# All transfers of a streaming kernel in one DMA queue

## The chip, the cores and the metric

The kernel runs on one core of a Trainium2 chip. The metric is the device time of one execution in microseconds (us), the median of several. A profile adds the span from the first to the last instruction, which is some 1.8 us shorter here. For one core the runs can't be sorted by comparing dies, so a run is called slow only when it is over 1.5% above the fastest of its kernel.

## The reference

The input is float32, 8 x 4096 x 2112. Groups of four neighbouring rows are averaged, and the average is subtracted from each of the four.

```
x_r = x.reshape(B, S // 4, 4, D)
pooled = x_r.mean(axis=2)
upsampled = np.repeat(pooled, 4, axis=1)
return x - upsampled
```

Every byte is read once and written once: 276.82 MB each way.

## The kernel before

A tile is 128 groups, one for each partition: 33,792 contiguous bytes a partition, 4.325 MB in all. There are 64 tiles and 6 slots in on-chip memory. A slot is loaded, changed in place by VectorE, and stored. SyncE issues all loads, ScalarE all stores, so there are two queues. Each issue can carry a wait, and an issuer stands still at it.

```
for k in range(n):                       # n = 64
    b, lap = k % SLOTS, k // SLOTS       # SLOTS = 6
    ...
    load = nc.sync.dma_start(out=slots[b][:], in_=xg[tile_rows])
    if lap:
        load._wait_ge(store_sems[b], 16 * lap)
    load.then_inc(load_sems[b], 16)

    add = nc.vector.tensor_add(out=s[:], in0=rows[:, 0, :], in1=rows[:, 1, :])
    add._wait_ge(load_sems[b], 16 * (lap + 1))
    ...                                  # two more adds, one fused multiply-add over the slot

    store = nc.scalar.dma_start(out=og[tile_rows], in_=slots[b][:])
    store._wait_ge(done_sem, done)
    store.then_inc(store_sems[b], 16)
```

## Time and profile before

| quantity | kernel before |
|---|---|
| time, median of 6 runs | 1286.78 us (1286.73 to 1287.18) |
| span of the profiled run | 1285.0 us |
| VectorE busy | 1026.5 us, 80% |
| two DMA queues, share of 16 engines | 50.0% and 49.9% |
| moved | 553.67 MB, 431 GB/s over the span |

Read it from the shares: the DMA engines are full and VectorE is not. The time of this kernel is the number of bytes over the rate of the DMA engines, as long as nothing lets those engines run dry. The prediction below shows the lines.

### The profile page before, as it was taken

The numbers are of one execution on the slowest core, as the hardware profiler recorded it, in microseconds if no ns is written. First come the engines' busy times: TensorE is split into PE (matmuls) and PEld (weight loads), VectorE is DVE, ScalarE is ACT, GpSimd is POOL, SyncE is SP. The second block draws the span as 40 slices with busy tenths as digits, with TensorE's granted clock in tenths as the row PEclk, the third lists the DMA queues.
The fourth block names the chain that finished last, engine by engine and source line by source line (L and its number), as shares of the span: only waits on it lengthen the run. The fifth ranks groups of instructions, "written<-read, shape, count | busy, mean of one in ns | idle before, by whom it ended". The sixth has DMA issues, their size and how long they took to land.

```text
span 1285.0 us, 439 instructions
## 1 busy us (share of the span) xinstructions
DVE 1026.5 (80%) x256; POOL 0.2 (0%) x4
## 2 busy tenths in 40 slices
DVE  5998778787787877878778788787887878878774
POOL 0000000000000000000000000000000000000000
DMA  9999999999999999999999999999999999999998
GB/s 404 421 438 432 426 438 437 430 429 437 437 431 429 437 437 431 429 437 437 431 429 437 437 431 429 437 436 430 430 438 434 429 432 438 434 428 433 438 434 374
DMA packets 18434, 553.67 MB, mean 431 GB/s; under 512 B 2048, under 2 KB 2048, under 8 KB 2048
## 3 DMA queue, kind: packets, MB, share of 16 engines
q1 hardware_dynamic: 9216, 276.83, 50.0%
q10 hardware_dynamic: 9216, 276.83, 49.9%
q14 instruction: 2, 0.02, 0.0%
HBM read 276.82 MB, written 276.82 MB: 431 GB/s over the span
## 4 chain that ended last, share of the span: by engine, by line
DVE 80%; another core or an unknown queue 17%; DMA 1%; issue 0%; SPq 0%
DVE slot L75 45%; DVE s_ps L71 12%; DVE s_sb L71 12%; DVE s_ps L66 6%; DVE s_sb L66 6%; DMA slot<-in_x_dram 1%; SPq L118 0%; SPq L53 0%
## 5 line engine op out<-in xcount | busy, mean ns | idle before, releaser
L75 DVE SCALAR_TENSOR_TENSOR slot<-s_sb,slot 128x8448 f32<-128x8448 f32 x32 | 286.7, 8958 | 1.1
L75 DVE SCALAR_TENSOR_TENSOR slot<-s_ps,slot 128x8448 f32<-128x8448 f32 x32 | 286.6, 8957 | 1.1
L66 DVE TENSOR_TENSOR s_sb<-slot 128x2112 f32<-128x2112 f32 x32 | 75.5, 2358 | 123.4 <-DMA slot<-in_x_dram 123.4
L66 DVE TENSOR_TENSOR s_ps<-slot 128x2112 f32<-128x2112 f32 x32 | 75.7, 2367 | 113.0 <-DMA slot<-in_x_dram 113.0
L71 DVE TENSOR_TENSOR s_ps<-s_ps,slot 128x2112 f32<-128x2112 f32 x64 | 151.4, 2366 | 2.2
L71 DVE TENSOR_TENSOR s_sb<-s_sb,slot 128x2112 f32<-128x2112 f32 x64 | 150.9, 2358 | 2.2
L107 POOL MEMSET const-uint8-127<- 128x1 uint8 x1 | 0.1, 102 | 0.0
L107 POOL MEMSET const-bfloat16-1.0<- 128x1 bf16 x1 | 0.1, 101 | 0.0
L107 POOL MEMSET const-float32-0.0<- 128x1 f32 x1 | 0.1, 98 | 0.2 <-issue 0.2
L107 POOL MEMSET const-float32-1.0<- 128x1 f32 x1 | 0.1, 98 | 0.0
## 6 DMA issues: line engine op xcount, KB each, us to landing
slot<-in_x_dram SPq DMA_DIRECT2D x64, 4224.0 KB, 59.7
out_dram<-slot ACTq DMA_DIRECT2D x64, 4224.0 KB, 43.9
```

The source lines that it names most:

```text
L66: add = nc.vector.tensor_add(out=s[:], in0=rows[:, 0, :], in1=rows[:, 1, :])
L71: add = nc.vector.tensor_add(out=s[:], in0=s[:], in1=rows[:, f, :])
L75: sub = nc.vector.scalar_tensor_tensor(out=rows, in0=s[:, None, :].to_broadcast([P, STRIDE, D]), scalar=-1.0 / STRIDE, in1=rows, op0=mybir ...
L107: nc = _bacc.Bacc("TRN2", target_bir_lowering=False, num_devices=1)
```

## The change

Its intent is to give the transfers one fixed order, store and load in turn, in place of leaving it to the engines how they mix two queues. SyncE issues everything. The load that refills a slot is put one store later than it could be: behind the store of tile k comes the load that waits for the store of tile k-1. The diff, with unchanged lines cut:

```diff
         done = 0
+        done_at = []
         for k in range(n):
...
-            load = nc.sync.dma_start(out=slots[b][:], in_=xg[tile_rows])
-            if lap:
-                load._wait_ge(store_sems[b], 16 * lap)
-            load.then_inc(load_sems[b], 16)
...
-            store = nc.scalar.dma_start(out=og[tile_rows], in_=slots[b][:])
-            store._wait_ge(done_sem, done)
+            done_at.append(done)
+
+        def load(k):
+            b, lap = k % SLOTS, k // SLOTS
+            dma = nc.sync.dma_start(out=slots[b][:], in_=xg[k * P:(k + 1) * P])
+            if lap:
+                dma._wait_ge(store_sems[b], 16 * lap)
+            dma.then_inc(load_sems[b], 16)
+
+        for k in range(SLOTS):
+            load(k)
+        for k in range(n):
+            b = k % SLOTS
+            store = nc.sync.dma_start(out=og[k * P:(k + 1) * P], in_=slots[b][:])
+            store._wait_ge(done_sem, done_at[k])
             store.then_inc(store_sems[b], 16)
+            if k and k - 1 + SLOTS < n:
+                load(k - 1 + SLOTS)
 
-        for b in range(SLOTS):
-            nc.sync.wait_ge(store_sems[b], 16 * len(range(b, n, SLOTS)))
+        for k in range(n - SLOTS, n):
+            nc.sync.wait_ge(store_sems[k % SLOTS], 16 * (k // SLOTS + 1))
```

More of the change, by code (lines that the diff above doesn't have):

```diff
@@ L58 @@
             s = s_ps if k % 2 else s_sb
-            tile_rows = slice(k * P, (k + 1) * P)
-            load = nc.sync.dma_start(out=slots[b][:], in_=xg[tile_rows])
-            if lap:
-                load._wait_ge(store_sems[b], 16 * lap)
-            load.then_inc(load_sems[b], 16)
             add = nc.vector.tensor_add(out=s[:], in0=rows[:, 0, :], in1=rows[:, 1, :])
```

## The prediction

> **What bounds the kernel now.** I read the page from the top, then asked the trace for the same quantities in stretches of the run. The first thing is the busy row and the row of the DMA engines.
>
> ```profile
> DVE 1026.5 (80%) x256; POOL 0.2 (0%) x4
> ...
> DMA  9999999999999999999999999999999999999998
> GB/s 404 421 438 432 426 438 437 430 429 437 437 431 429 437 437 431 429 437 437 431 429 437 437 431 429 437 436 430 430 438 434 429 432 438 434 428 433 438 434 374
> ```
>
> VectorE is busy for 80% of the span and never full after the opening. The 16 DMA engines are at 90% or more in 39 of the 40 slices; only the first and the last slice move visibly less (404 and 374 GB/s). So the kernel streams, and VectorE is hidden behind the stream. The table of queues says who uses the engines:
>
> ```profile
> q1 hardware_dynamic: 9216, 276.83, 50.0%
> q10 hardware_dynamic: 9216, 276.83, 49.9%
> ...
> HBM read 276.82 MB, written 276.82 MB: 431 GB/s over the span
> ```
>
> q1 is SyncE's queue (the loads), q10 ScalarE's (the stores). Together their packets fill 99.9% of 16 engines for 1285.0 us: there is almost no idle engine time to win. Each queue has 9216 packets for 64 transfers; 128 rows of 33,792 bytes times 64 are 8192 data packets, and the other 1024 are 16 small semaphore packets for each transfer. One data packet takes about 0.500 x 16 x 1285.0 / 8192 = 1.255 us by this line (1.251 us in the packet records themselves, the same for loads and stores). An engine carries 8192 x 2 / 16 = 1024 of them, so 1024 x 1.251 = 1281 us of pure transfer in a span of 1285.0 us.
>
> The decisive view is the table of stretches, because the kernel already shows, at its two ends, what one queue alone can do. Columns are the stretch, its length, busy VectorE, busy GpSimd, clock, share of the DMA engines, GB/s:
>
> ```profile
> 14.00:29.00 15.00, 14.90 (x4) 0.00 (x0) 1.00 1.01 437
> 62.00:1253.40 1191.40, 962.09 (x240) 0.00 (x0) 1.00 1.00 433
> 1253.40:1278.00 24.60, 16.06 (x4) 0.00 (x0) 1.00 1.01 437
> ```
>
> From 14 to 29 us only loads run (the first store is issued at 29.51 us). From 1253.4 us only stores run: the last tile's first add starts at 1253.41 us, when the last load has landed. Both stretches, one queue each with several transfers end to end, show 437 GB/s; the middle with both queues shows 433. These figures count a packet whole in one stretch, so a short window is uncertain by a few GB/s. I read all three as one rate. A single queue, loads only or stores only, loses nothing at the joints between transfers.
>
> Last, the waits of the DMA issuers and the times to landing:
>
> ```profile
> SPq L61 <- DMA out_dram<-slot: 1170.2, 58, 50.6
> ...
> slot<-in_x_dram SPq DMA_DIRECT2D x64, 4224.0 KB, 59.7
> out_dram<-slot ACTq DMA_DIRECT2D x64, 4224.0 KB, 43.9
> ```
>
> SyncE spends 1170 us waiting for stores to free slots, 58 times, once for every load after the first six. This is no loss: a load takes 59.7 us from issue to landing and a transfer needs 4.325 MB / 433 GB/s = 10.0 us of all engines, so several transfers always stand in line. The wait is the queue being full.
>
> **What the Trainium skill says.** "DMA: Bandwidth & Descriptors", section "Issuing engines are not separate DMA queues": DMAs started by different engines run on the same 16 DMA engines, and several issuers save only the sequencer's issue time. The trace agrees: issuing is 0.33 us of a 20 us tile period, and one queue or two show 437 and 433 GB/s. The same page, "Where 436 GB/s comes from", gives 435.2 GB/s as the fabric's ceiling; the 433 here is within 1% of it. Its section "Queues, rings and completion order" says that an engine takes turns between queues by packet, takes one queue's descriptors in order, and that the semaphore increment is a write that lands only after that engine's earlier writes. The last could stall a queue; the stores-only stretch at 437 GB/s shows no such stall between stores. "HBM Reference", section "Specifications (TRN2)", says a core streaming alone is bounded by its 16 DMA engines, near 425 GB/s; this trace is a little above.
>
> **The change part by part.**
> Removed: 64 store issues from ScalarE. Added: the same 64 on SyncE, 0.34 us each, 22 us over the run on an engine that waits 1170 us. They cost nothing on the path. Bytes, packets and VectorE's 256 instructions are the same.
> Moved: order. SyncE now issues L0 to L5, S0, S1, L6, S2, L7, S3, L8 and so on, and stands still at whichever waits first: a store waits for VectorE, load k+5 for store k-1 to land. The question is whether the queue ever drains while SyncE stands still.
>
> Opening: the six loads run until 1.0 + 48 x 1.251 = 61 us. A tile takes VectorE 3 x 2.36 + 8.96 = 16.05 us, and the first result is ready at 29.5 us as now, so S0 is issued at 29.5 and S1 at 45.6 us, both before the loads end. S0 runs from 61 to 71, S1 to 81. Load 0's data take about 11 us and the first add starts at 13.34 us, so I estimate some 1.5 us from last byte to waiter. L6 is then issued at about 72.6, while S1 still has 8 us to run; S2 (ready since 61.6) follows it at once. No gap.
>
> Steady state: call t the moment when S(k-1) ends. The order S(k-2), L(k+3), S(k-1), L(k+4), S(k) puts S(k-2)'s end at t - 20. L(k+4) and S(k) are issued 1.5 us after that, at t - 18.5, while L(k+3) and S(k-1) are still in line. So the queue holds at least 18 us of work when new work comes. VectorE has tile k loaded at t - 70 and done by about t - 52, some 34 us before its store can be issued; it never holds SyncE up. Of a 20 us period it has 4 us free, as now.
>
> Tail: the last load goes before five stores, 50 us before the end. VectorE needs 16 us for it, so its store is ready long before its turn. Now, the last store is issued at 1269.6 us, while the one before is still running.
>
> The sum: at 433 GB/s the 553.65 MB take 1278.6 us. The other 6.4 us of the span are the first packets (0 to 10 us at 324 GB/s: 10 x (1 - 324/433) = 2.5 us), a small dip when the stores set in (29 to 62 us at 418 GB/s: 1.1 us), and the end (1270 to 1285 us at 324 GB/s: 3.8 us), rounded. The first is unchanged, since the same six loads are issued first. The dip may go, move or stay. Of the end, the data stop near 1282 us and the rest is the last receipt and the closing of the program, which the change keeps. So about 1 us can be won, and about as much lost. Reported time is 1.8 us above the span (1286.81 against 1285.0). I predict **1286.5 us**.
>
> **The rivals.**
> (a) Turning from load to store within one queue costs something. In the opening dip some 30 packets of q1 took 2.1 instead of 1.25 us, 0.85 us more. If every engine paid 0.85 us at each of some 120 turns, the time would rise by 102 us to about 1389 us. Against it: in the middle each engine already mixes equal numbers of load and store packets, and practically all take 1.251 us.
> (b) The semaphore write behind a store holds up the load behind it in the same queue. With two queues the other would fill that gap. At an estimated 1.5 us (the landing time above) for each of 58 joints this is 87 us, 1374 us. Against it: the stores-only tail passes such joints at full rate. But a store followed by a load in one queue is seen nowhere in this trace, so it isn't closed.
> (c) Head-of-line blocking: SyncE waits for one thing while another could go. For it: one issuer, two kinds of waits, both in strict order. Against it: 18 us in line and 34 us slack at VectorE. If the slack were wrong by a whole tile, VectorE (1026 us plus two unhidden ends) would come near the bound, some per cent slower.
> (d) Faster: fewer turns between reads and writes at the memory. The unmixed stretches read 437 against 433, at most 1% or 12 us, inside the counting error. The packet time is the same to the nanosecond in both, so I give it little.
>
> **Range and chances.** Runs before lie within 0.5 us. The floor of 1281 us plus start and receipt keeps the time above about 1284; small stalls from (a) or (b) would add a few us. Range 1284.5 to 1290. Beyond 2% slower (1312.5) only (a), (b) or (c) in full reach: 5% together. Faster by 2% would need 443 GB/s: 1%.
>
> **What would show it.** In the changed kernel's table of queues one queue should have 18,432 packets, 553.65 MB and about 99.9%; the table of stretches 433 GB/s through the middle; VectorE still 1026 us with waits of about 3.8 us for each tile. Times to landing show the new order: loads about 30 us (three transfers), stores about 40 us (four). SyncE's waits should still name stores, near 19 us each. Wrong by (a): longer packets at equal engine share and lower GB/s. By (b): a share well under 99%, with VectorE idle longer. By (c): SyncE waiting on VectorE and the DMA row below 9.

## The result, and the profile after

| | before | after |
|---|---|---|
| time, median of 6 runs each | 1286.78 us | 1288.27 us (1287.65 to 1289.08) |
| ratio of fast runs, 95% interval | | 1.0011 (0.9998 to 1.0024) |
| span of the profiled run | 1285.0 us | 1286.2 us |

The time is the same within 2%. A ratio here is the mean time of one kernel's fast runs over that of the other's of the same rounds, so it isn't quite the ratio of the medians.

The page of the changed kernel, the lines that answer to those of the prediction:

```profile
DVE 1026.0 (80%) x256; POOL 0.2 (0%) x4
...
DMA  9999999999999999999999999999999999999998
GB/s 404 420 433 430 430 435 433 432 432 435 434 433 432 433 435 434 433 431 435 434 432 432 435 434 432 431 433 435 435 432 432 434 435 431 432 435 435 431 433 372
...
q1 hardware_dynamic: 18432, 553.66, 99.9%
...
slot<-in_x_dram SPq DMA_DIRECT2D x64, 4224.0 KB, 29.9
out_dram<-slot SPq DMA_DIRECT2D x64, 4224.0 KB, 39.5
```

The row of DMA engines is the same, digit by digit, and one queue now holds what two held: 18,432 packets at 99.9%. Only the times to landing moved: loads from 59.7 to 29.9 us, stores from 43.9 to 39.5 us. They are times of standing in line. A shorter line with the same throughput moves no more data.

The waits of the issuer, after (waiter, what it waited for: total us, times, longest):

```profile
SPq L86 <- DMA out_dram<-slot: 1111.1, 58, 28.4
SPq L95 <- DVE slot L70: 85.5, 5, 25.7
```

SyncE waited 1111.1 / 58 = 19.2 us for each store, a little under one tile period of 20.0 us. It waited for VectorE only 5 times: twice at the opening, for the first two stores, while the first six loads were still running, and for the last three stores, issued at 1211.24, 1231.23 and 1251.17 us, when no load was left to issue. The last store came into line some 23 us before its turn, so this cost nothing.

The opening dip of the stream is still there, but later. The stretches before, then after:

```profile
29.00:62.00 33.00, 32.79 (x10) 0.00 (x0) 1.00 0.99 418
62.00:102.00 40.00, 39.16 (x12) 0.00 (x0) 1.00 1.00 433
```

```profile
29.00:62.00 33.00, 32.79 (x10) 0.00 (x0) 1.00 1.03 430
62.00:102.00 40.00, 39.69 (x12) 0.00 (x0) 1.00 0.97 418
62.00:1253.40 1191.40, 977.80 (x244) 0.00 (x0) 1.00 1.00 433
```

Before, stores join the loads at 29.5 us and the dip is there. After, the first store stands behind six loads and runs from some 61 us on, and the dip follows it. Over the middle the changed kernel holds 433 GB/s, as the kernel before does.

### The profile page after: what moved, and what is told of

It reads as the page before. It is cut to its first block, busy times and chain, and to the rows that moved or that the text cites. A ratio compares the mean times of both kernels' runs of the same rounds, so it can differ in the third digit from the quotient of the medians.

```text
span 1286.2 us, 437 instructions
## 1 busy us (share of the span) xinstructions
DVE 1026.0 (80%) x256; POOL 0.2 (0%) x4
## 3 DMA queue, kind: packets, MB, share of 16 engines
q1 hardware_dynamic: 18432, 553.66, 99.9%
## 4 chain that ended last, share of the span: by engine, by line
DMA 90%; DVE 7%; SPq 1%; issue 0%
DMA out_dram<-slot 86%; DVE slot L70 3%; DMA slot<-in_x_dram 3%; DVE s_ps L66 1%; DVE s_sb L66 1%; SPq L86 1%; DVE s_ps L61 1%; DVE s_sb L61 1%; SPq L128 0%; SPq L53 0%
## 6 DMA issues: line engine op xcount, KB each, us to landing
slot<-in_x_dram SPq DMA_DIRECT2D x64, 4224.0 KB, 29.9
out_dram<-slot SPq DMA_DIRECT2D x64, 4224.0 KB, 39.5
```

## The experiments

The theory: 16 DMA engines stream at one rate, whichever queue feeds them and in whichever order, as long as work stands in line. In one queue, what keeps work in line is where the waits sit in the order. The rivals from the prediction are that a turn between store and load costs time (a), that a semaphore write behind a store holds up its queue (b), that one wait in strict order blocks work that could go (c), and that one queue is faster (d).

### Is the 1.5 us real, and does the queue or a longer line matter? (e1, e3, e4)

e1 is the changed kernel again. e3 puts the load one store later still:

```diff
-            if k and k - 1 + SLOTS < n:
-                load(k - 1 + SLOTS)
+            if k >= 2 and k - 2 + SLOTS < n:
+                load(k - 2 + SLOTS)
```

e4 issues everything, the last waits too, from ScalarE:

```diff
-            dma = nc.sync.dma_start(...)
+            dma = nc.scalar.dma_start(...)
-            store = nc.sync.dma_start(...)
+            store = nc.scalar.dma_start(...)
```

> The changed kernel once more, to size a difference of about 0.1%. My theory (the 16 DMA engines stream at one rate whichever queue feeds them) expects a ratio of 1.000 to 1.002 to the kernel before, spans of 1285.5 to 1287.5 us. If the 1.5 us between the first medians was only the spread of runs, the interval should include 1.000 with a ratio below 1.0005; if it is real, the interval should lie above 1.0005.

> One queue, the load of tile k+4 behind the store of tile k (waits for the store two tiles back): more work in line. My theory expects no change: 1287 to 1289 us, DMA share 99.9%. If the last 1.5 us of the changed kernel come from a line that is sometimes nearly dry, this one should give them back, 1286.8 us.

> The changed kernel with all transfers and the last waits on ScalarE in place of SyncE. My theory expects the same as the changed kernel, 1287 to 1289 us, with all 18432 packets in q10. If SyncE's queue had something special, this one should differ by more than 2 us.

Measured, 5 runs each: e1 1288.15 us (1287.70 to 1288.55), e3 1288.07 us (1287.33 to 1290.51), e4 1288.20 us (1287.22 to 1288.92), beside 1286.83 us (1286.71 to 1287.16) of the kernel before. Ratios are 1.0009, 1.0012 and 1.0009, each with an interval from about 0.9997 to about 1.0023. So the interval does not separate one queue from two, and e1 fits neither of the two outcomes named before it: its ratio is above 1.0005, its interval includes 1.000. But of 15 one-queue runs none is as fast as the slowest of the 9 runs of the kernel before beside them: some 1.3 us are probably real, a tenth of a per cent. A longer line does not give them back (e3), and they don't belong to SyncE's queue (e4).

Where they sit can be seen at the end of the span. The kernel before, then the changed one; the last column is GB/s:

```profile
1281.00:1282.00 1.00, 0.00 (x0) 0.00 (x0) 1.00 0.09 34
1282.00:1283.00 1.00, 0.00 (x0) 0.00 (x0) 1.00 0.00 0
```

```profile
1281.00:1282.00 1.00, 0.00 (x0) 0.00 (x0) 1.00 0.24 101
1282.00:1283.00 1.00, 0.00 (x0) 0.00 (x0) 1.00 0.24 101
1283.00:1284.00 1.00, 0.00 (x0) 0.00 (x0) 1.00 0.08 34
```

34 GB/s in 1 us is one packet of 33,792 bytes. Before, one engine brings its last packet after 1281 us. After, several engines are still at work until past 1283 us: a few are late, not the stream as a whole. The records of single packets say more: after 100 us, 2 data packets of the kernel before took over 1.27 us, but 24 in the changed kernel, 60 in e1, 65 in e3 and 56 in e4. Many of them, above all early on, lie near the moments at which the queue turns between store and load. Worked out as an average over 16 engines, they add 0.5 to 0.8 us in place of 0.1 us, about half of what is to be explained. The rest is that the engines drift apart, and the end waits for the last of them. Each engine writes the semaphore once behind its part of a transfer, so these 16 writes show the spread. In the changed kernel they lie 0.7 us apart for the first loads, 2.8 us in the middle and 3.3 us for the last store (3.2 to 3.6 us in e1, e3 and e4); in the kernel before it is 0.4, 1.0 and 1.8 us. For the last store the first write comes at 1281.30 us, against 1281.20 us before, the last at 1284.58 us against 1282.99 us. Why an engine is now and then late at a turn is not shown, and stays open.

### Does the order matter at all? (e2)

e2 takes the shift by one store away: the load that refills slot k stands directly behind the store of tile k.

```diff
-            if k and k - 1 + SLOTS < n:
-                load(k - 1 + SLOTS)
+            if k + SLOTS < n:
+                load(k + SLOTS)
```

> One queue, but the load of tile k+6 stands directly behind the store of tile k and waits for it to land, so the later stores stand behind that wait. My theory (what keeps one queue full is the work already in line when SyncE stands still, which the shift by one tile in the diff gives) expects the line to run dry at each store: 2.5 to 3.5 us of landing and new start at each of 58 tiles, 1430 to 1490 us, and a DMA share near 87%. The rival (the order of issue in one queue does not matter, because the engines are the limit) expects 1286 to 1290 us.

Measured: 1511.77 us, ratio 1.1752 (1.1734 to 1.1770). The rival falls: order matters much. My size was too small (1430 to 1490 us), and so was the share (near 87%). The lines of e2's page and a piece of its timeline (start, length, engine, line, what):

```profile
span 1511.1 us, 437 instructions
...
q1 hardware_dynamic: 18432, 553.66, 92.3%
```

```profile
599.50 0.33 SPq L86 DMA_DIRECT2D slot<-in_x_dram  x1
599.88 0.43 SPq L95 DMA_DIRECT2D out_dram<-slot  x1
...
623.07 0.33 SPq L86 DMA_DIRECT2D slot<-in_x_dram  x1
623.44 0.43 SPq L95 DMA_DIRECT2D out_dram<-slot  x1
```

Load and store are issued as a pair, then nothing for 23.6 us until that store has landed. By then the queue is empty. The cost is 1511.1 - 1286.2 = 225 us, or 3.9 us for each of 58 refills. The share splits it: the engines' idle time rose from 0.1% of 1286.2 us to 7.7% of 1511.1 us, by 115 us, and their busy time from 1285 to 1395 us, by 110 us, although the bytes are the same. So each dry spell costs about 2.0 us of idle engines and another 1.9 us in which packets are in flight but take longer. I had counted only the first kind. The packet records after 100 us say where the second kind lies, as an average over the engines: about 0.6 us in the first packets after the restart, and 1.3 us some 8 to 11 us later, in the last packets of the load, before the store behind it begins. In this run the turn from load to store is not free. The run also shows that a busy share of DMA engines can hide a loss: 92.3% sounds better than 366 GB/s is.

This shows what the diff's "k - 1" does. With it, a store and a load stand in line while SyncE waits; the timeline of the changed kernel has the first refill issued while the second store still runs:

```profile
74.42 0.34 SPq L86 DMA_DIRECT2D slot<-in_x_dram  x1
74.80 0.63 SPq L95 DMA_DIRECT2D out_dram<-slot  x1
...
84.47 0.34 SPq L86 DMA_DIRECT2D slot<-in_x_dram  x1
```

The second refill could only be issued 10.05 us later, when the second store had landed: that store followed the first at full rate, so the line was never dry between.

### Does a turn cost, or a joint? (e5, e6, e11)

Each transfer is cut into four, one for each of the four rows of a group. In e5 the four stores of a tile are issued in a row, then the four loads. In e6 they alternate. Each quarter has a store semaphore of its own, and VectorE waits for all four loads. From e5 to e6 the edit is:

```diff
             more = k and k - 1 + SLOTS < n
             for f in range(STRIDE):
                 store(k, f)
-            for f in range(STRIDE):
                 if more:
                     load(k - 1 + SLOTS, f)
```

> One queue, each transfer cut into four of 8448 bytes a row, stores of a tile in a group of four, then the loads in a group of four: four times the transfers, joints and semaphore writes, four times the packets, but as many turns between store and load as the changed kernel has (some 120). My theory expects 433 GB/s and at most 1% over the changed kernel, 1288 to 1300 us. If the semaphore write behind a store held the queue up by even 0.2 us, 192 more joints behind stores would add some 38 us: 1326 us or more.

> The same quarters, but store and load alternate quarter by quarter: the same packets and semaphore writes as the grouped one, four times its turns (some 470). My theory (a turn costs nothing) expects the time of the grouped one within 3 us. The rival (each turn costs 0.85 us, the excess of the slow packets at the first turn) expects 350 turns more, 300 us more, about 1590 us; a turn cost of 0.05 us would show as 18 us.

Measured, 4 runs each: grouped 1303.78 us (1303.49 to 1304.14), ratio 1.0132; mixed 1303.28 us (1303.02 to 1303.98), ratio 1.0129. About 350 more turns moved the time by -0.5 us. Once the line runs steadily a turn costs nothing that can be measured, and rival (a) falls for this kernel. It is no rule for every turn. At the first turn of the changed kernel the 16 packets that start from 61.4 to 61.8 us, one for each engine, took 1.9 to 2.4 us in place of 1.25, and in e2 the turns cost 1.3 us each (above). Why a turn costs time there and not in steady running is not shown.

Both lie some 15 us above the changed kernel, a little more than I allowed, and their pages give 425 GB/s over the span in place of 430. Is that the packets, or joints in one queue? e11 cuts the kernel before, with its two queues, into the same quarters:

```diff
-            load = nc.sync.dma_start(out=slots[b][:], in_=xg[tile_rows])
+            for f in range(STRIDE):
+                cols = slice(f * D, (f + 1) * D)
+                load = nc.sync.dma_start(out=slots[b][:, cols], in_=xg[tile_rows, cols])
```

with the stores cut likewise on ScalarE.

> The kernel before, two queues, with each transfer cut into the same four quarters as in the one-queue runs, which took 1303.3 and 1303.8 us. If the 15.5 us there come from the fourfold packets themselves, two queues pay them too: 1301 to 1304 us. If they come from joints that only a single queue can't hide, this run stays at 1286 to 1290 us.

Measured: 1304.99 us (1304.78 to 1305.21), ratio 1.0141. Two queues pay it too, and a little more: 18.2 us over the kernel before of the same rounds. So the cost comes with the finer cut and not from the one queue, and rival (b) falls: 384 more joints in one queue cost no more than in two. e6 says it more directly, since its loads stand behind stores four times as often as those of e5, in the same time. Per engine the cut adds 3072 data packets; 15.5 us over 3072 is about 5 ns each, and 18.2 us about 6 ns, if it is all put on them. Here one queue is even 1.2 to 1.7 us faster than two (in other rounds), the reverse of the 1.3 us seen with whole transfers: these runs show no general lead of either.

### How many slots does each order need? (e7, e8, e12, e9, e10)

The edit is one number, in the changed kernel (e7, e9) or in the kernel before (e8, e12, e10):

```diff
-SLOTS = 6
+SLOTS = 3        # e9 and e10: 2
```

> The changed kernel with 3 slots in place of 6. My working: tile k is loaded 10 us before store k-1 ends, VectorE and the landing take 17.5 us, and load k+1 still runs until 10 us after that end, so store k comes some 2.5 us before the line is dry: 1287 to 1310 us, with SyncE now waiting mostly on VectorE. If the slack were a tile smaller than worked out, 10 us or more a tile would be lost: 1900 us or more.

> The kernel before with 3 slots. A slot needs load + landing + 16 us of VectorE + store + landing; three slots in 60 us leave 44 us less some 4 us for two transfers, 20 us each, which is the rate of shared engines: 1287 to 1310 us. Beside the one-queue kernel with 3 slots it tells whether the two orders need slots alike.

> The kernel before with 3 slots once more, because its four runs spread from 1316 to 1354 us where the one-queue kernel with 3 slots stayed within 1.5 us. If the spread belongs to the two queues sharing engines, it comes again: a range of over 15 us around 1335 us. If it was chance, the runs agree within 5 us.

> The changed kernel with 2 slots. My theory of the line: the load of tile k is the last work in line, and store k waits for its landing and VectorE, so the period is load 10 + landing and VectorE 17.5 + new start 1 + store 10 = 38.5 us, 64 times: 2400 to 2560 us, DMA share near 52%. The rival (one queue costs nothing however few slots there are) expects 1290 us.

> The kernel before with 2 slots. The two slots can run half a period apart: one loads or stores while the other is on VectorE, slot period 10 + 17.5 + 10 + 3 = 40.5 us and two tiles in it: 1300 to 1450 us, well under the one-queue kernel with 2 slots. If one queue and two behave alike here, it is 2400 us or more.

| slots | one queue | two queues |
|---|---|---|
| 6 | 1288.27 us | 1286.78 us |
| 3 | 1333.94 us (1333.67 to 1335.11) | e8: 1337.27 us (1316.50 to 1354.49, two of four slow), e12: 1340.01 us (1329.05 to 1342.95) |
| 2 | 2448.49 us (one run, state unknown) | 1520.54 us (one run, state unknown) |

With 3 slots both lose some 3 to 4%, more than I expected (up to 1310 us). SyncE now waits on VectorE and hardly on anything else, as expected:

```profile
SPq L95 <- DVE slot L70: 1267.1, 64, 27.1
SPq L102 <- DMA out_dram<-slot: 11.0, 1, 11.0
```

The 2.5 us of lead that I worked out for a store was too little: e7's engine share is 98.8% of 1333.3 us, so by the same sum as for e2 some 15 us are idle engines and 32 us longer packets. The line is just dry, or nearly, and three quarters of the extra time of the longer packets lies in the last packet of a transfer, as at the turns of e2. The fast ratio of one queue is 1.0368. The two-queue kernel gives different times from run to run (two of e8's four runs count as slow, at the same clock as the others; its fast ratio is 1.0283, e12's 1.0416): 26 us between its seven fast runs, 38 us between all nine, against 1.4 us for one queue. e12's own range is 13.9 us, between the 5 us and the 15 us that I had named, so it decides nothing by itself. I can't rank the two at 3 slots. That a fixed order makes the time repeatable fits this, but only this.

With 2 slots the order decides. The timeline of the one-queue kernel with 2 slots:

```profile
623.87 0.33 SPq L95 DMA_DIRECT2D out_dram<-slot  x1
624.24 0.43 SPq L86 DMA_DIRECT2D slot<-in_x_dram  x1
646.21 2.37 DVE L61 TENSOR_TENSOR s_ps<-slot 128x2112 f32<-128x2112 f32 x1 [22.37 <-DMA slot<-in_x_dram]
...
662.40 0.33 SPq L95 DMA_DIRECT2D out_dram<-slot  x1
662.77 0.43 SPq L86 DMA_DIRECT2D slot<-in_x_dram  x1
```

The period is 662.40 - 623.87 = 38.53 us; I had worked out 38.5. The sum came out so well partly by luck: the landing in it was too long by about 1.1 us (1.5 against 0.4 us, see below), and slow packets, 0.9 us in this period, nearly all at the turn, which it left out, made up for that. A store goes, a load behind it, VectorE waits 22.37 us for that load, and the next store waits for VectorE while nothing is in line. Two queues let load and store go as each is ready, and take 1520.54 us, slower than I expected (at most 1450) but far below 2448. So rival (c) is a true mechanism: while SyncE stands at a store that waits for VectorE, the load behind it can't go. With 6 slots slack hides it. What was run is one queue in this order, with the shift by one store; one queue without the shift was not tried with 2 slots, so the 2448 us belong to this order and not to every single queue.

## Why the prediction was right

The chance of 94% on "same" (what its 5% and 1% leave) and the range of 1284.5 to 1290 us hold; the measured 1288.27 us lies 1.8 us above the number.

- **The bound.** Right. 99.9% of 16 engines before and after, and VectorE unchanged.
- **One queue streams as well as two.** Right. Its evidence, the loads-only and stores-only stretches, did not contain a store followed by a load in one queue. e5, e6 and e11 close that for a line in steady running: there neither turns nor joints cost anything of note. In a line that runs dry again and again, e2 shows 1.3 us at each turn from load to store, which the prediction had seen only once, at the opening.
- **The line never drains.** Right, and the times to landing (30 and 40 us predicted, 29.9 and 39.5 measured) and the waits (near 19 us predicted, 19.2 measured) show that the order runs as worked out. e2 shows that this was the step that mattered: without the shift the same one queue costs 17.5%.
- **A landing of 1.5 us.** Too long. The first refill was issued at 74.42 us and not at 72.6 us, but not because the landing took longer: the last semaphore write of the first store is at 74.06 us, 0.36 us before that issue. (For load 0 it is 13.10 us, and the first add starts at 13.46 us.) It was the transfers that ended later. The first packets start 1.0 us after their issue and take some 1.9 us, those before the first store some 2.2 us, and so the six loads end at 64.1 us and not at 61 us. The prediction had taken this slow start for a part of the landing. The line had room for it.
- **At most about 1 us either way.** The term was a little small and had no sign: some 1.3 to 1.5 us were lost, by engines that drift apart during the run, and seen at the end. I had looked for a loss at the opening, and that dip only moved. The sum behind the term doesn't close either: its pieces 2.5, 1.1 and 3.8 us make 7.4 us and not 6.4. The rounding of 433 GB/s covers the difference (433.5 would give 1277.2 us in place of 1278.6), but it is as large as the effect in question.
- **The rivals.** (a) and (b) fall by experiment, for a line in steady running. (c) is real but hidden by six slots: with 2 slots it nearly doubles the time. The 3 to 4% at 3 slots can't be put on it, since two queues lose as much. (d) found nothing.

## What to carry to other kernels

When the DMA engines are full before and after, moving transfers between queues moves waiting time and not throughput; first look for a stretch of the trace where one queue already works alone. When all transfers share one issuer, work out for each wait how much is still in line while the issuer stands at it, and put the refill of a slot behind at least one more store, or each tile pays for the line that ran dry, 3.9 us here. With few slots be wary of one issuer in strict order, since it can hold back work that could go; of the two orders tried with 2 slots, the one with two queues was far the faster.

## What the Trainium skill lacked or had wrong

- "DMA: Bandwidth & Descriptors", section "Issuing engines are not separate DMA queues", says that several issuers save only the issue time. For throughput with a full line the runs agree (1288.27 against 1286.78 us). It lacks that a second issuer also lets waits pass each other: with 2 slots two issuers take 1520.54 us and one, in the order of this change, takes 2448.49 us.
- The same page, section "Anatomy of one DMA — SWDGE (gpsimd) path", gives a fixed cost of about 2.0 us for a DMA of that path, which is not the one used here. Here a queue that runs dry costs 3.9 us each time, about 2.0 us of idle engines and 1.9 us of longer packets, at the restart and at the turn after it; the first part is of the page's size, and the second is not on any page that I read.
- The same page, section "Why small descriptors are slow (HBM only)", gives a fixed overhead of about 3 cycles for each packet, and works it out for 256 bytes. It has no measured time for packets as large as these; going from 33,792 to 8,448 bytes cost 15.5 us with one queue and 18.2 us with two, about 5 to 6 ns for each added packet of an engine, if all of it is put on them.
- "HBM Reference", section "Specifications (TRN2)", gives about 425 GB/s for a core that streams alone. This core holds 433 GB/s, loads and stores mixed.
